# Token sums of the last group's first eight v columns added two steps later in banks of their own, gathered passes spread over four more steps, first weights loaded later

## The chip, the cores and the metric

One core of a Trainium2 chip runs the whole program. The metric is device time in microseconds (us) for one execution; the number that counts is the median of several runs. Engines are named as in the profile: PE (TensorE matmul), PEld (its weight load), DVE (VectorE), ACT (ScalarE), POOL (GpSimd), SP (SyncE, which only issues DMAs here).

## What is computed

The program is one layer of a hybrid decoder for 512 prompt tokens and 64 sample tokens, width 2048. The first half (modulation, input projection, recurrences, output projection) is not touched by the change. The second half is the expert layer: every token scores 8 heads of 128x128 product keys, takes the top 16 of 16384 experts per head, and each expert is one row of `peer_u` and one row of `peer_v`.

```python
eidx = jnp.take_along_axis(cidx, pos, axis=-1)          # 8 heads x 16 experts per token
g = jax.nn.softmax(top, axis=-1).astype(xb.dtype)
act = jax.nn.gelu(jnp.einsum('td,thkd->thk', xb, expert_u[eidx])) * g
return jnp.einsum('thk,thkd->td', act, expert_v[eidx])
...
x = x + gate2[:, None, :] * peer(h2, peer_wq, peer_sub_keys, peer_u, peer_v)
...
y_prompt = rmsnorm(xp, final_g)
```

## The kernel before: staging, queues and the order of the work

**Two ways to an expert.** The 128 blocks of 128 experts are ranked by how often the prompt uses them. The 80 most used blocks (`L = 80`) are computed densely: for every block, all 512 prompt tokens against all 128 experts, with the weight zero where a token did not choose an expert. Picks in the other blocks, and all picks of the 64 sample tokens, are *gathered*: a row of 2048 numbers per token is fetched by an indirect DMA on POOL (`take`, L1548) and DVE multiplies and adds it. The gathered picks are held as lists of columns: column j of a list holds one expert row for each of up to 128 tokens, so one *pass* is one 1 MB fetch and one DVE instruction over 128x2048 elements. There are 223 passes over `u` and 223 over `v` (lists of 64, 37, 23, 40, 33 and 26 columns, `GT`). In each `v` list DVE adds up in PSUM (`accB`, L1604), the last pass writes the finished token sums into SBUF (L1606), and an indirect DMA on POOL writes them to the DRAM tensor `accd` (L1615; the sample tokens' sums go to `accs`).

**U half.** Steps n = 0 to 159, two per dense block: PE multiplies the block's `u` weights with the tokens (24 matmuls of 512 columns a step, `u_half`, L1712). The weights come in as fp32 (`raw`, an SP DMA) and are split into a high part (`xhi`, ACT, L1202) and a low part (`xlo`, POOL, L1203); three matmuls per product follow. In the same half POOL writes the dense weights of the choice to DRAM (`gd`, L1933) and ACT writes the activations (`actd`). `E0 = 146` is the step at which the buffers of this part are handed over and the first two weight groups are read back: `load_group` (`actr`, POOL, L1654) and `load_weights` (`gsb`, POOL, L1659); DVE multiplies the two (`weigh`, L1664) and splits the product (`halve`, L1686, ACT L1682).

**V half.** The 80 dense blocks are taken in groups of 8 (nine of them) and two of 4. A step m (0 to 79) is four blocks times one quarter of the 2048 output columns, that is four columns of 128 (kq = 0 to 3), each 12 matmuls into one PSUM bank (`v_column`, L1735). There are four such banks. In a group of 8 a column needs two steps, and after the second DVE adds the bank to `acc` (`v_sum`, L1759); in the groups of 4 (steps 72 to 75 and 76 to 79) it does so after each step. Each step needs two 512 KB loads of `v` weights (SP, `raw`), two splits on ACT and POOL, and, per four blocks, one `load_weights`, `load_group`, `weigh` and `halve`. Every engine runs its queue in order, so a DVE pass that waits for its rows holds up the adds behind it, and PE then has no free bank.

**How the passes are spread.** `last` is M - VQ - ENDS = 80 - 4 - 5 = 71. The 213 `v` passes that are left after ten early ones are spread over steps 0 to 70 by a budget: every column gets room of 2.37, or 1.62 where its step ends a sum, and less in the first four steps (`room`), and `gather_to` emits as many passes as the budget has reached. Passes near a list's end count for less (down to 0.35), so they come closer together.

**The end.** At step 72 the writes to `accd` are flushed. At step 75 four rows `tok` (1 MB each) are loaded from `accd` on SP. In the last group (steps 76 to 79) each column's bank gets four more matmuls against the identity (L1739) that turn the token rows and add them, and `v_sum` then multiplies by the gate and adds (L1761), ACT squares (L1765), SP stores the column (L1766), DVE adds the square (L1771). `add_x` (L1750) adds the residual `xf` to `acc` one step ahead of that. `finish_b` (L1796 on) finishes the 64 sample tokens in pieces at the steps of `fplan`: load `tokb` and `x2b`, 16 matmuls into a PSUM tile `ph` of four banks (L1808), norm, store. After step 79 comes the final norm (`token_norm`, L1782 and L1787) and the output (L2140).

Of the kernel before, what the change touches and what calls it, by code (L numbers as in the profile page):

```python
# [81 lines left out]
def build(ctx, tc, A, O, dbg=None):  # L82
# [1640 lines left out]
    def v_column(n, gi, q, bl, first, last, kq):  # L1723
# [6 lines left out]
        for j, i in enumerate(bl):  # L1730
# [3 lines left out]
            for a, (st, mv) in enumerate(((hi, ah), (hi, al), (lo, ah))):  # L1734
                PE.matmul(pv, st, mv, start=first and j == 0 and a == 0,  # L1735
                          stop=last and not end and j == SG - 1 and a == 2)
        if end:
            for t in range(QT):
                PE.matmul(pv[:, t * 128:(t + 1) * 128], fin["tok"][t][:, k * 128:(k + 1) * 128], ident,  # L1739
                          start=False, stop=t == QT - 1)  # L1740
# [11 lines left out]
    scaled_early = (1, 4, 7, 10, 13)  # L1752

    def v_sum(gi, k, pv):
        ak = acc[:, k, :]
        if gi == 0:
            S.activation(ak, pv, AF.Copy)
        elif gi < len(GROUPS) - 1:
            V.tensor_add(ak, ak, pv)  # L1759
        else:  # L1760
            V.scalar_tensor_tensor(ak, pv, g2[:, k, 0:1], ak, op0=ALU.mult, op1=ALU.add)  # L1761
            if k == 0:
                fin["t"] = [actp.tile([128, NA], F32, name=f"sqs{i}", tag="act") for i in range(3)]
            sq = fin["t"][1]
            S.activation(sq, ak, AF.Square)  # L1765
            nc.sync.dma_start(x2d[:, k, :], ak)  # L1766
            if k == 0:
                fin["sq"] = fin["t"][0]
                V.tensor_copy(fin["sq"], sq)
            else:  # L1770
                V.tensor_add(fin["sq"], fin["sq"], sq)  # L1771
            e = k - 2 if k == KD - 1 else k - 3
            if e in scaled_early:
                S.activation(acc[:, e, :], acc[:, e, :], AF.Copy, scale=cols[:, C_FG + e:C_FG + e + 1])
# [312 lines left out]
    for m in range(M):  # L2087
# [6 lines left out]
        if m == last + 1:  # L2094
            flush(1 << 30)
        if m == last + 4:
            fin["tok"] = []
            for t in range(QT):
                r = new_row(f"tok{t}")[0]
                nc.sync.dma_start(r, accd[t * 128:(t + 1) * 128, :])  # L2100
# [177 lines left out]
```

## Time and profile before

| what | us |
|---|---|
| median of three runs | 3108.51 (3106.38 to 3116.51) |
| the profiled execution, its own time | 3115.26 |
| its span in the profile | 3113.5 |
| U half, first to last matmul of L1712 | 1141.1 to 2143.7 |
| V half, steps 0 to 71 | 2143.56 to 2974.21 |
| steps 72 to 75 | 2974.21 to 3022.42 |
| steps 76 to 79 and their token matmuls | 3022.42 to 3089.35 |
| final norm and output | 3089.35 to 3113.5 |

The profiled execution is 6.75 us above the median of the runs and inside their spread. Times in the profile count from the span's start. A step's bounds are the start of its first matmul and that of the next step's, counted off in the timeline (24 matmuls a U step, 48 a V step). Busy PE time includes the modelled ends of pipelined matmuls, so the length of a step says more than its busy share.

### The profile page before, as it was taken

The numbers are of one execution on the slowest core, as the hardware profiler recorded it, in microseconds if no ns is written. First come the engines' busy times: TensorE is split into PE (matmuls) and PEld (weight loads), VectorE is DVE, ScalarE is ACT, GpSimd is POOL, SyncE is SP. The second block draws the span as 40 slices with busy tenths as digits, with TensorE's granted clock in tenths as the row PEclk, the third lists the DMA queues.
The fourth block names the chain that finished last, engine by engine and source line by source line (L and its number), as shares of the span: only waits on it lengthen the run. The fifth ranks groups of instructions, "written<-read, shape, count | busy, mean of one in ns | idle before, by whom it ended". The sixth has DMA issues, their size and how long they took to land.

```text
span 3113.5 us, 49239 instructions
## 1 busy us (share of the span) xinstructions
PE 2996.4 (96%) x18521; PEld 2549.6 (82%) x18521; DVE 2229.6 (72%) x3414; ACT 1051.1 (34%) x1675; POOL 1764.6 (57%) x1071
## 2 busy tenths in 40 slices
PE   5899999999999999999999999989999999999997
PEld 3688888899999998877888888878887878777776
DVE  5456532144356899988899999867788898888855
ACT  3244412123243232323655655623322222122222
POOL 2133333344313336666677777768777787777842
PEclk9999999999999999999999999999999999999998
DMA  9844466644433238999879999999999997999963
GB/s 368 297 139 138 170 205 210 223 164 161 140 113 97 75 93 290 317 350 367 315 286 396 383 401 366 376 363 381 396 410 411 410 374 280 388 371 376 371 204 143
DMA packets 238900, 880.89 MB, mean 283 GB/s; under 512 B 36246, under 2 KB 37142, under 8 KB 178102
## 3 DMA queue, kind: packets, MB, share of 16 engines
q0 software_dynamic: 78096, 475.29, 38.2%
q1 hardware_dynamic: 148896, 381.17, 34.9%
q10 hardware_dynamic: 11664, 21.24, 1.8%
q8 instruction: 146, 2.39, 0.3%
q14 instruction: 98, 0.80, 0.1%
HBM read 878.84 MB, written 65.76 MB: 303 GB/s over the span
## 4 chain that ended last, share of the span: by engine, by line
PE 55%; DMA 11%; DVE 5%; issue 3%; POOL 2%; ACT 0%; SPq 0%; POOLq 0%; DVEq 0%; ACTq 0%
PE pu L1712 26%; PE pv L1735 14%; DMA raw<-vq 8%; PE pp_o L148 6%; PE qb L148 3%; PE qa L148 2%; PE gbank L1921 1%; DMA v<-v,rows 1%; DVE accB L1604 1%; POOL xlo L1203 1%; PE gx L1921 1%; DMA u<-u,rows 1%; POOL v L1548 1%; PE pv L1739 0%; DMA tok<-accd 0%
## 5 line engine op out<-in xcount | busy, mean ns | idle before, releaser
L1203 POOL TENSOR_TENSOR xlo<-raw,xhi 128x1024 fp32r<-128x1024 f32 x320 | 796.0, 2495 | 300.9 <-ACT xhi L1202 297.6
L1202 ACT ACTIVATE xhi<-raw 128x1024 fp32r<-128x1024 f32 x320 | 338.1, 1060 | 777.0 <-PE pv L1735 293.1
L1604 DVE SCALAR_TENSOR_TENSOR accB<-v,dots,accB 128x2048 f32<-128x2048 f32 x211 | 496.4, 2353 | 124.7 <-DMA v<-v,rows 122.8
L1576 DVE SCALAR_TENSOR_TENSOR u<-u,hT 128x2048 f32<-128x2048 f32 x223 | 504.1, 2283 | 103.6 <-DMA u<-u,rows 103.0
L1735 PE MATMUL pv<-ahi,xhi 128*128 128x512 f32 x1280 | 506.8, 396 | 30.1 <-DVE acc L1759 24.2
L1712 PE MATMUL pu<-hhi,xhi 128*128 128x512 f32 x1280 | 508.9, 398 | 0.7 <-ACT qt L1228 0.7
L1712 PE MATMUL pu<-hhi,xlo 128*128 128x512 f32 x1280 | 500.6, 391 | 8.8 <-POOL xlo L1203 8.8
L1735 PE MATMUL pv<-ahi,xlo 128*128 128x512 f32 x1280 | 503.2, 393 | 1.2 <-POOL xlo L1203 1.2
L1735 PE MATMUL pv<-alo,xhi 128*128 128x512 f32 x1280 | 503.5, 393 | 0.2 <-DVE alo L1686 0.2
L1712 PE MATMUL pu<-hlo,xhi 128*128 128x512 f32 x1280 | 500.9, 391 | 0.0
L1548 POOL DMA_INDIRECT u<-u,rows x223 | 226.8, 1017 | 166.3 <-DVE u L1576 120.8
L1735 PEld LDWEIGHTS pv<-ahi,xhi 128*128 128x128 f32 x1280 | 243.4, 190 | 86.8 <-issue 16.2
L1712 PEld LDWEIGHTS pu<-hhi,xlo 128*128 128x128 f32 x1280 | 241.7, 189 | 61.6 <-POOL xlo L1203 10.5
L1548 POOL DMA_INDIRECT v<-v,rows x223 | 258.1, 1158 | 59.9 <-issue 40.9
L1712 PEld LDWEIGHTS pu<-hhi,xhi 128*128 128x128 f32 x1280 | 241.5, 189 | 56.7 <-issue 1.6
L1735 PEld LDWEIGHTS pv<-ahi,xlo 128*128 128x128 f32 x1280 | 243.2, 190 | 53.5 <-POOL xlo L1203 2.0
L1735 PEld LDWEIGHTS pv<-alo,xhi 128*128 128x128 f32 x1280 | 243.6, 190 | 50.3 <-DVE alo L1686 0.6
L1712 PEld LDWEIGHTS pu<-hlo,xhi 128*128 128x128 f32 x1280 | 241.7, 189 | 47.7
L872 POOL TENSOR_TENSOR wlo_q<-raw_q,whi_q 128x1024 fp32r<-128x1024 f32 x30 | 73.3, 2443 | 174.9 <-ACT whi_q L871 161.2
L1915 ACT ACTIVATE op<-op,it 128x128 f32<-128x128 f32 x512 | 155.2, 390 | 0.0
L1715 ACT ACTIVATE act<-pu 128x512 f32<-128x512 f32 x80 | 47.9, 598 | 296.4 <-PE pu L1712 282.8
L137 POOL TENSOR_TENSOR wlo_o<-raw_o,whi_o 128x1024 fp32r<-128x1024 f32 x31 | 75.1, 2423 | 111.8 <-ACT whi_o L135 99.2
(566 smaller groups left out, 5616.9 us busy)
## 6 DMA issues: line engine op xcount, KB each, us to landing
wa<-w_ada SPq DMA_DIRECT2D x96, 1024.0 KB, 7.0
raw<-ut SPq DMA_DIRECT2D x160, 512.0 KB, 7.8
raw<-vq SPq DMA_DIRECT2D x320, 256.0 KB, 18.8
gd<-stg POOLq DMA_DIRECT2D x64, 320.0 KB, 11.7
gsb<-gd POOLq DMA_DIRECT2D x20, 1024.0 KB, 10.3
actd<-act ACTq DMA_DIRECT2D x76, 256.0 KB, 7.8
actr<-actd POOLq DMA_DIRECT2D x19, 1024.0 KB, 13.0
raw_o<-w_out SPq DMA_DIRECT2D x32, 512.0 KB, 3.6
```

Of the source, the lines that this page charges most:

```text
L137: lo_engine(share).tensor_sub(lo, raw, r32(hi))
L148: PE.matmul(o, st, mv[pick](k), start=first, stop=last)
L872: G.tensor_sub(lo, qraw.pop(j), r32(hi))
L1202: S.activation(hi, raw, AF.Copy)
L1203: G.tensor_sub(lo, raw, r32(hi))
L1548: G.indirect_dma_start(out=out, out_offset=None, in_=src, in_offset=bass.IndirectOffsetOnAxis(ap=idx, axis=0), bounds_check=NE * 128 - 1, ...
L1576: V.scalar_tensor_tensor(r, r, 1.0, st["h"], op0=ALU.mult, op1=ALU.mult, accum_out=dots[i][:, j:j + 1])
L1604: V.scalar_tensor_tensor(st["a"], r, dots[i][:, j:j + 1], st["a"], op0=ALU.mult, op1=ALU.add)
L1712: PE.matmul(pu, st[:, kk, :], movA[mv](k), start=k == 0 and a == 0, stop=k == KD - 1 and a == 2)
L1735: PE.matmul(pv, st, mv, start=first and j == 0 and a == 0, stop=last and not end and j == SG - 1 and a == 2)
L1915: S.activation(ops[:, j0 + j, :], ops[:, j0 + j, :], AF.Copy, scale=it[2][:, b * 4 + j:b * 4 + j + 1])
L1921: PE.matmul(pg[a:a + 64, j * L:(j + 1) * L], ops[:, j0 + j, a:a + 64], wr[:, j0 + j, :], start=True, stop=True)
```

## The change: what it does

- `ENDS` goes from 5 to 1, so `last` is 75: the same 213 passes are spread over steps 0 to 74.
- `LATE_K = 8`: in the last group the first eight columns (steps 76 and 77) no longer get token matmuls; their bank is multiplied by the gate and added at once. Two steps later, beside column k (8 to 15), the token rows of column k - 8 are turned into a bank of `ph` of their own, and both columns are finished one after the other (new function `finished`).
- The `tok` loads move from the start of step 75 to step 76, kq 2; the flush of the writes to `accd` from the start of step 72 to step 75, kq 2. `fplan` moves the six pieces of `finish_b` from steps 72 to 75 to steps 75 to 77.
- The columns are squared, scaled and stored in the order 8, 0, 9, 1 and so on (`order`).
- `load_weights(0)` moves from E0 + 1 to E0 + 3.

```diff
-ENDS = 5
+ENDS = 1
+LATE_K = 8
...
-                          stop=last and not end and j == SG - 1 and a == 2)
-        if end:
+                          stop=last and not (end and k >= LATE_K) and j == SG - 1 and a == 2)
+        if end and k >= LATE_K:
             for t in range(QT):
                 PE.matmul(pv[:, t * 128:(t + 1) * 128], fin["tok"][t][:, k * 128:(k + 1) * 128], ident,
                           start=False, stop=t == QT - 1)
+            e = k - LATE_K
+            for t in range(QT):
+                PE.matmul(fin["ph"][:, kq * NA + t * 128:kq * NA + (t + 1) * 128],
+                          fin["tok"][t][:, e * 128:(e + 1) * 128], ident, start=True, stop=True)
...
-    scaled_early = (1, 4, 7, 10, 13)
+    order = [e for k in range(LATE_K, KD) for e in (k, k - LATE_K)]
+    scaled_early = [order[j] for j in (1, 4, 7, 10, 13)]
...
+        elif k < LATE_K:
+            V.scalar_tensor_tensor(ak, pv, g2[:, k, 0:1], ak, op0=ALU.mult, op1=ALU.add)
         else:
...
+            finished(k, pv)
+            b = k % (KD // VQ)
+            finished(k - LATE_K, fin["ph"][:, b * NA:(b + 1) * NA])
+
+    def finished(k, src):
+        ak = acc[:, k, :]
+        V.scalar_tensor_tensor(ak, src, g2[:, k, 0:1], ak, op0=ALU.mult, op1=ALU.add)
+        j = order.index(k)
+        if j == 0:
+            fin["t"] = [actp.tile([128, NA], F32, name=f"sqs{i}", tag="act") for i in range(3)]
+        sq = fin["t"][1]
+        S.activation(sq, ak, AF.Square)
+        nc.sync.dma_start(x2d[:, k, :], ak)
+        if j == 0:
+            fin["sq"] = fin["t"][0]
+            V.tensor_copy(fin["sq"], sq)
+        else:
+            V.tensor_add(fin["sq"], fin["sq"], sq)
...
-        for sg, o in ((0, 1), (1, 7)):
+        for sg, o in ((0, 3), (1, 7)):
...
-    fplan = {(last + 1, 2), (last + 2, 3), (last + 3, 1), (last + 3, 3), (last + 4, 1), (last + 4, 3)}
+    fplan = {(last, 3), (last + 1, 0), (last + 1, 2), (last + 2, 0), (last + 2, 1), (last + 2, 3)}
...
-        if m == last + 1:
-            flush(1 << 30)
-        if m == last + 4:
-            fin["tok"] = []
-            for t in range(QT):
-                r = new_row(f"tok{t}")[0]
-                nc.sync.dma_start(r, accd[t * 128:(t + 1) * 128, :])
-                fin["tok"].append(r)
         for kq in range(KD // VQ):
+            if (m, kq) == (last, 2):
+                flush(1 << 30)
+            if (m, kq) == (last + 1, 2):
+                fin["tok"] = []
+                for t in range(QT):
+                    r = new_row(f"tok{t}")[0]
+                    nc.sync.dma_start(r, accd[t * 128:(t + 1) * 128, :])
+                    fin["tok"].append(r)
```

Where the instructions stand is set by a scheduler from the order in which the code emits them, so three places of it follow. In the changed kernel line numbers are one higher up to the change and more behind it.

**POOL, U half, around step E0.** `gd` is the last write of the dense weights, `gsb` the first read of them, `xlo` the low parts that PE waits for, `u` gathered rows. Before:

```order
L1933 DMA gd<-stg_20286 128x5x128
L1203 TENSOR_TENSOR xlo_20745<-raw_20686,xhi_20744 128x1024
L1548 DMA u_20_20748<-u,rows_9005 128x2048
L1659 DMA gsb_20780<-gd 128x2048
L1203 TENSOR_TENSOR xlo_20788<-raw_20739,xhi_20787 128x1024
L1548 DMA u_21_20791<-u,rows_9005 128x2048
L1548 DMA u_22_20796<-u,rows_9005 128x2048
L1654 DMA actr_20826<-actd 128x2048
L1203 TENSOR_TENSOR xlo_20834<-raw_20782,xhi_20833 128x1024
```

In the changed kernel, from the same low part on:

```order
L1204 TENSOR_TENSOR xlo_20745<-raw_20686,xhi_20744 128x1024
L1549 DMA u_20_20748<-u,rows_9005 128x2048
L1204 TENSOR_TENSOR xlo_20786<-raw_20739,xhi_20785 128x1024
L1549 DMA u_21_20789<-u,rows_9005 128x2048
L1549 DMA u_22_20794<-u,rows_9005 128x2048
L1655 DMA actr_20824<-actd 128x2048
L1204 TENSOR_TENSOR xlo_20832<-raw_20780,xhi_20831 128x1024
L1549 DMA u_23_20835<-u,rows_9005 128x2048
L1660 DMA gsb_20867<-gd 128x2048
L1204 TENSOR_TENSOR xlo_20875<-raw_20826,xhi_20874 128x1024
```

The read `gsb` stood two rows behind the low part `xlo_20745`, ahead of the next low part; now it stands eight rows behind it, two low parts and three more gathers later.

**DVE, the last passes.** `accB` and `v_25` are passes of the last list, `pv` with its column the banks that are added. Before, around the end of step 71 (columns 12 to 15 of group 8) and the start of step 72 (columns 0 on of group 9):

```order
L1604 SCALAR_TENSOR_TENSOR accB_27369<-v_24_28070,dots_20213,accB_27369 128x2048
L1606 SCALAR_TENSOR_TENSOR v_25_28088<-v_25_28088,dots_20213,accB_27369 128x2048
L1664 TENSOR_TENSOR actr_27905<-actr_27905,gsb_27809 128x2048
L1759 TENSOR_TENSOR acc<-acc,pv_12_28075 128x512
L1759 TENSOR_TENSOR acc<-acc,pv_13_28093 128x512
L1759 TENSOR_TENSOR acc<-acc,pv_14_28108 128x512
L1686 TENSOR_TENSOR alo_28177<-actr_27905,ahi_28176 128x2048
L1759 TENSOR_TENSOR acc<-acc,pv_15_28124 128x512
L1759 TENSOR_TENSOR acc<-acc,pv_0_28246 128x512
L1759 TENSOR_TENSOR acc<-acc,pv_1_28260 128x512
```

In the changed kernel, steps 73 to 75 of group 9 (columns 6 and 7, 8 to 11, 12):

```order
L1765 TENSOR_TENSOR acc<-acc,pv_6_28346 128x512
L1605 SCALAR_TENSOR_TENSOR accB_27651<-v_21_28230,dots_20213,accB_27651 128x2048
L1765 TENSOR_TENSOR acc<-acc,pv_7_28365 128x512
L1765 TENSOR_TENSOR acc<-acc,pv_8_28405 128x512
L1605 SCALAR_TENSOR_TENSOR accB_27651<-v_22_28263,dots_20213,accB_27651 128x2048
L1765 TENSOR_TENSOR acc<-acc,pv_9_28420 128x512
L1605 SCALAR_TENSOR_TENSOR accB_27651<-v_23_28322,dots_20213,accB_27651 128x2048
L1765 TENSOR_TENSOR acc<-acc,pv_10_28435 128x512
L1605 SCALAR_TENSOR_TENSOR accB_27651<-v_24_28341,dots_20213,accB_27651 128x2048
L1607 SCALAR_TENSOR_TENSOR v_25_28360<-v_25_28360,dots_20213,accB_27651 128x2048
L1765 TENSOR_TENSOR acc<-acc,pv_11_28453 128x512
L1765 TENSOR_TENSOR acc<-acc,pv_12_28493 128x512
```

The last pass `v_25` stood ahead of the adds of step 71; now it stands in step 74, ahead of the add of column 11. Nine passes, `v_17` to `v_25`, stand behind the first add of step 72, where there were none.

**SP, the last loads.** `raw` are `v` weights, `tok` the token rows, `tokb` and `x2b` the inputs of `finish_b`, `xf` the residual. Before, at step 75:

```order
L1191 DMA raw_28523<-vq 128x512
L2100 DMA tok_28532<-accd 128x2048
L2100 DMA tok_28534<-accd 128x2048
L2100 DMA tok_28536<-accd 128x2048
L2100 DMA tok_28538<-accd 128x2048
L1819 DMA y<-x2b 2048x1x64
L1746 DMA xf_28590<-x1d 128x4x512
```

In the changed kernel, at steps 75 and 76:

```order
L1192 DMA raw_28484<-vq 128x512
L1814 DMA tokb<-accs 128x2048
L1819 DMA x2b<-x1d 128x16x64
L1751 DMA xf_28545<-x1d 128x4x512
L1176 TENSOR_LOAD blk
L1192 ISA
L1192 DMA raw_28570<-vq 128x512
L1176 TENSOR_LOAD blk
L1192 ISA
L1192 DMA raw_28570<-vq 128x512
L2116 DMA tok_28630<-accd 128x2048
L2116 DMA tok_28632<-accd 128x2048
```

The four token rows stood behind the last weights but one; now they stand behind the last weights, and `tokb`, which had been loaded in step 72, stands ahead of those. On PE the 16 matmuls of `ph` from `tokb` stood between columns 6 and 7 in step 73; now they stand between the last column of step 75 and the first of step 76. On ACT the last high parts (`xhi`) stood between the squares of the last group; now all stand ahead of the first square.

More of the change, by code (lines that the diff above doesn't have):

```diff
@@ L1759, in v_sum @@
             V.tensor_add(ak, ak, pv)
-        else:
[L1761 to L1774, printed above, removed]
+        elif k < LATE_K:
+            V.scalar_tensor_tensor(ak, pv, g2[:, k, 0:1], ak, op0=ALU.mult, op1=ALU.add)
+        else:
+            finished(k, pv)
[15 more added lines that the diff above has]
+            V.tensor_add(fin["sq"], fin["sq"], sq)
+        e = order[j - 2 if j == KD - 1 else j - 3] if j >= 3 else None
+        if e in scaled_early:
+            S.activation(acc[:, e, :], acc[:, e, :], AF.Copy, scale=cols[:, C_FG + e:C_FG + e + 1])
     def token_norm(sq, n, nm, pool, banks):
@@ L1805, in finish_b @@
         yield
-        ph = psum["p"].tile([128, D], F32, name="ph", tag="hT", bufs=1)
+        ph = fin["ph"] = psum["p"].tile([128, D], F32, name="ph", tag="hT", bufs=1)
         for k in range(KD):
@@ L2133, in build @@
     R = drive(token_norm(fin["sq"], NA, "a", vp, banks))
-    for k in range(KD):
+    for k in order:
         ak = acc[:, k, :]
```

## The prediction

> **What bounds the kernel now.** I read the page first (the busy slices), then the windows of the V half step by step, then who waited for whom in it, then the timeline around the two stretches that the change touches beside it, and the chain at the end. From the page:
>
> ```profile
> PE   5899999999999999999999999989999999999997
> DMA  9844466644433238999879999999999997999963
> ```
>
> PE looks full nearly everywhere, and DMA is full from slice 23 to 33, which is the V half. Busy PE hides waits, so the lengths of steps decide. Windows (length, then busy time and count of PE, PEld, DVE, ACT and POOL, granted clock, DMA share, GB/s) over steps 0 to 71, steps 4 to 7, 16 to 19, 44 to 47, 64 to 67, 72 to 75 and 76 to the last matmul:
>
> ```profile
> 2143.56:2974.21 830.65, 799.18 (x3457) 654.60 (x3456) 700.63 (x385) 197.26 (x185) 640.95 (x401) 0.99 0.96 375
> 2188.46:2231.98 43.52, 43.52 (x194) 36.04 (x192) 30.43 (x13) 16.32 (x18) 36.54 (x23) 1.00 0.99 384
> 2319.00:2365.00 46.00, 43.91 (x194) 35.99 (x193) 40.35 (x21) 9.94 (x9) 36.26 (x23) 1.00 1.02 411
> 2636.26:2691.30 55.04, 46.57 (x193) 36.71 (x192) 46.64 (x27) 11.65 (x12) 41.61 (x27) 0.95 0.97 369
> 2885.33:2930.69 45.36, 44.00 (x192) 35.97 (x193) 43.17 (x26) 12.50 (x11) 37.14 (x25) 1.00 1.01 406
> 2974.21:3022.42 48.21, 48.21 (x229) 39.94 (x228) 24.22 (x32) 12.03 (x14) 21.49 (x10) 1.00 0.61 191
> 3022.42:3089.35 66.93, 61.80 (x321) 52.65 (x319) 36.18 (x44) 16.79 (x24) 15.10 (x6) 0.95 0.48 165
> ```
>
> An undisturbed step takes 43.52 / 4 = 10.88 us. Steps 0 to 71 took 830.65 where 72 x 10.88 = 783.4 would do: 47.3 us lost. Of the eighteen windows of four steps, ten are over 45 us long, spread from steps 16 to 19 to steps 64 to 67 (the first and the last are quoted, and the longest); the others are at the floor or within 1.4 us of it. Why PE stands, from the waits of PE and DVE over that stretch (us in total, times, longest), and the passes and adds themselves from the groups by line (count, busy, mean ns, idle before):
>
> ```profile
> PE pv L1735 <- DVE acc L1759: 24.2, 12, 5.1
> ```
> ```profile
> DVE accB L1604 <- DMA v<-v,rows: 116.9, 83, 5.8
> ```
> ```profile
> L1604 DVE SCALAR_TENSOR_TENSOR accB<-v,dots,accB 128x2048 f32<-128x2048 f32 x204 | 480.0, 2353 | 118.7 <-DMA v<-v,rows 116.9
> L1759 DVE TENSOR_TENSOR acc<-acc,pv 128x512 f32<-128x512 f32 x127 | 84.3, 679 | 5.9 <-PE pv L1735 5.6
> ```
>
> DVE is busy for 700.63 us and waits 116.9 us for gathered rows: together 817.5 of 830.65. PE waits for the adds, the adds stand behind passes, passes wait for rows, and rows wait for a DMA that runs at a share of 1.02. So passes per step are what this stretch is paid in. In steps 72 to 75, where no pass is left, DVE is free for 24 of 48 us and DMA at 0.61.
>
> **Part 1: nine passes leave steps 0 to 71.** The budget gives 4 x 2.37 = 9.48 to a step that ends no sum and 6.48 to one that does; over 71 steps that is 558.5, and the four new ones (71 to 74, all ending a sum) add 25.9. 213 x 25.9 / 584.4 = 9.4 passes; in the order it is nine, `v_17` to `v_25`. A pass costs DVE 2.353 us plus 116.9 / 204 = 0.57 us of waiting, 2.93 us. Were all nine on the path, 26.3 us would go. But in eight of eighteen windows PE lost little or nothing, so a pass less is worth nothing there: 26.3 x 10 / 18 = 14.6. From below: near a list's end passes come closer together, and it is these bursts that make the longest windows. By the budget the ten long windows hold 123 passes before, and 121 after, because the bursts fall on other steps: 2 x 2.93 = 6 us. I take **-15** (6 to 26): the even part of the load falls everywhere, and DVE's queue carries over from step to step. Nothing is paid for the nine at their new place: 9 x 2.353 = 21 us of passes in steps 72 to 74 meet 24 us of idle DVE, and `finish_b` and its DVE work have left as well; without that cover it would be up to the 26 again.
>
> **Part 2: the first weights.** Windows of the U steps 149, 150 and 151 (the last undisturbed, 5.44 us), then the timelines of POOL and of ACT there:
>
> ```profile
> 2070.81:2080.73 9.92, 7.37 (x26) 5.57 (x25) 6.66 (x7) 1.06 (x1) 4.12 (x3) 0.83 0.82 321
> 2080.73:2094.60 13.87, 8.06 (x26) 6.13 (x24) 6.37 (x7) 1.65 (x2) 9.78 (x8) 0.75 0.77 281
> 2094.60:2100.04 5.44, 5.44 (x26) 4.51 (x24) 3.71 (x4) 1.06 (x1) 4.95 (x4) 1.00 0.86 307
> ```
> ```profile
> 2070.63 0.91 POOL L1933 DMA_DIRECT2D gd<-stg  x1
> 2071.56 2.36 POOL L1203 TENSOR_TENSOR xlo<-raw,xhi 128x1024 fp32r<-128x1024 f32 x1
> ...
> 2084.15 0.56 POOL L1659 DMA_DIRECT2D gsb<-gd  x1 [9.04 <-DMA gd<-stg]
> 2084.73 2.36 POOL L1203 TENSOR_TENSOR xlo<-raw,xhi 128x1024 fp32r<-128x1024 f32 x1
> ```
> ```profile
> 2074.26 1.06 ACT L1202 ACTIVATE xhi<-raw 128x1024 fp32r<-128x1024 f32 x1 [5.79 <-DMA raw<-ut]
> ...
> 2082.50 1.06 ACT L1202 ACTIVATE xhi<-raw 128x1024 fp32r<-128x1024 f32 x1 [0.98 <-DMA raw<-ut]
> ```
>
> POOL stood 9.04 us at the read `gsb`, until `gd` had landed, with the next low part behind it: its high part was ready at 2075.3, it ran at 2084.73. Step 150 lost 13.87 - 5.44 = 8.4 us by that. In the new order two low parts and three gathers come first; the second of these waits for the high part of 2082.50, so POOL reaches `gsb` at about 2087, after the 2084.15 at which `gd` was there. The wait goes. What is late next is a load: the weights for step 152 are asked for when the low part of 2071.56 ends (2073.9), the ones before came in 16.5 us (asked for at 2066, there at 2082.5), so theirs are in at 2090.4, the low part 3.5 us later, where PE would be at about 2092: some 2 us. **-6.4** (-3 to -9).
>
> **Part 3: the end.** SP's timeline, the DMA issues (KB each, median us to landing), and pieces of the chain (start, us):
>
> ```profile
> 3013.12 4.04 SPq L1191 DMA_DIRECT2D raw<-vq  x4
> 3017.34 2.06 SPq L2100 DMA_DIRECT2D tok<-accd  x4
> ```
> ```profile
> xf<-x1d SPq DMA_DIRECT2D x4, 1024.0 KB, 5.2
> tok<-accd SPq DMA_DIRECT2D x4, 1024.0 KB, 10.0
> ...
> tokb<-accs SPq DMA_DIRECT2D x1, 1024.0 KB, 8.2
> ```
> ```profile
> 2993.41 3.52 PE ph L1808 x32
> ...
> 3018.71 12.87 DMA tok<-accd
> ...
> 3032.42 5.12 PE pv L1735 x12
> ...
> 3038.54 2.77 PE pv L1735 x12
> 3041.31 0.89 PE pv L1739 x8
> ...
> 3089.38 0.76 DVE acc L1761
> ```
>
> A column with its token matmuls takes 2.73 + 0.89 = 3.63 us, 16 of them 58.0; 66.93 - 58.0 = **8.9** us went on waiting for `tok` in step 76 and on the slow matmuls behind that wait (12 in 5.12 us, not 2.77). This goes: in the change the token rows are asked for some 4.5 us into step 76, need about 14 us (3017.34 to 3031.6), and PE wants them two steps after 76, one column in, over 24 us after its start. The 128 token matmuls stay 128, only placed in 78 and 79. `finish_b`'s PE work (3.52 and about 1 us) moves from steps 73 to 75 to 76 and 77: 0 in sum. New are three things. (a) `tokb` is now asked for behind the loads of step 75, 6.4 us after its start by the rows above (3017.34 against 3010.92), and PE's queue has its matmuls at 10.88. With 8.2 us to landing it is in at 14.6: **+3.7**; with the 5.2 of `xf`, 0.7; with the 10.0 of `tok`, 5.5. (b) the sample norm's square root stands behind two high parts on ACT at the start of step 77, and PE has a matmul for it one column in: 0 to 2 us, **+1**. (c) DVE's tail. One finished column now and its neighbours, from the timeline:
>
> ```profile
> 3042.24 0.75 DVE L1761 SCALAR_TENSOR_TENSOR acc<-pv,mod,acc 128x512 f32<-128x512 f32 x1 [0.79 <-PE pv L1739]
> ...
> 3043.08 0.63 ACT L1765 ACTIVATE sqs<-acc 128x512 f32<-128x512 f32 x1 [3.03 <-DVE acc L1761]
> ...
> 3043.74 0.69 DVE L1771 TENSOR_TENSOR sqs<-sqs,sqs 128x512 f32<-128x512 f32 x1 [0.76 <-ACT sqs L1765]
> 3044.35 0.75 DVE L1750 SCALAR_TENSOR_TENSOR acc<-acc,mod,xf 128x512 f32<-128x512 f32 x1
> ```
>
> A column occupies DVE from 3042.24 to 3044.35, 2.11 us. In steps 78 and 79 PE takes 2.73 + 2 x 0.89 = 4.5 us a column, DVE two finishes, 4.2, and in step 78 also an `add_x` of 0.7: DVE falls 1.6 us behind in step 78 and regains 1.2 in step 79. After PE's last matmul one finish is left as before, plus what the pair adds: the first of the two starts 0.9 us before PE ends and takes 2.1, so **+1.2** (0 to 4). Sum of part 3: -8.9 + 3.7 + 1 + 1.2 = **-3.0** (-8 to +3).
>
> Two rules of the Trainium skill bear on (a). The page TensorE: Matmul & The Clock Gate (Part 1) says that the array's clock falls to half once PE has idled for a window of about 3.4 us: the trace agrees where PE waited in U steps 149 and 150 (granted 0.83 and 0.75) and in the 5.12 us above; by it a wait of 3.7 us could cost another 5.12 - 2.77 = 2.4 us, and part 3 would be -0.6. The page DMA: Bandwidth & Descriptors (Anatomy of one DMA) gives about 2.0 us plus the bytes over 436 GB/s, an estimated 4.4 us for the 1 MB of `tokb`, and part 3 would be -6.7; the 8.2 us measured for this very transfer decides against it.
>
> **Sum.** -15 - 6.4 - 3.0 = -24.4. The profiled execution took 3115.26 us, 1.76 more than its span; 3115.26 - 24.4 = 3090.9. It is 6.75 above the median, which I take as run-to-run, so the same terms on the median: 3108.5 - 24.4 = **3084**.
>
> **Rivals.**
>
> - *The bursts decide, not the sum.* PE's 24.2 us on adds came in 12 waits, and the budget's 121 against 123 passes speak for it; the DMA share of 1.02 in the even windows (16 to 19, 64 to 67) against it. Part 1 is 0: 3108.5 - 9.4 = 3099.
> - *All nine passes count*, and `tokb` comes in time: DVE's 817.5 of 830.65 us speaks for it, the windows at the floor against it. -26.3 - 8.4 - 6.7 = -41.4: 3067.
> - *Slower: the nine passes wait at the end.* In steps 72 to 75 every step ends a sum, so PE needs all four adds within a step, and each now stands behind passes; POOL's write to `accd`, with two low parts behind it, waits for the last pass as well. If each pass waits the longest time seen, 5.8 us, 52 us of waiting meet 24 us of idle DVE: +28 us of standing PE. Rows that are so late pay nothing earlier either (part 1 is 0): 3108.5 - 9.4 + 28 = 3127. It turns slower from a mean wait of (24 + 9.4) / 9 = 3.7 us; the mean of the 83 waits is 1.4, and DMA has room there (0.61).
> - *That the change does not do what it says* is excluded by the order: passes, token matmuls and loads stand where the text puts them.
>
> **The numbers.** Forecast 0.67, bursts 0.16, all nine 0.12, slower 0.05. The range 3070 to 3102 takes in the bursts' case and leaves out the two ends. A difference under 0.3% (9.3 us, about the spread of the three runs) can't be told from none. Faster by more than that (under 3099.2): the forecast but for its upper end, all nine, and half the bursts' case: 0.81. Within it 0.14, slower 0.05.
>
> **What the profile after would show.** Right: the windows over steps 0 to 71 together some 15 us shorter, at the same 10.88 us floor; no `gsb` wait on POOL, U step 150 under 8 us; steps 72 to 75 at about 43.5 us; no wait for `tok` in the last group, a wait of PE before the `ph` matmuls of `tokb`, steps 78 and 79 at 18.1 us each. Wrong: long windows of the same total length on other steps; DVE waiting over 3 us a pass in steps 72 to 74; PE waiting for `tok` in step 78; DVE over 5 us behind PE at the end.

## The result, and the profile after

The changed kernel took 3088.05 us (median of five runs, 3086.14 to 3096.41), the kernel before beside it 3108.51 (five runs, 3103.28 to 3116.51): a ratio of 0.9935, with a 95% interval of 0.9913 to 0.9957. The forecast was 3084. The profiled execution took 3086.14 us, 1.9 below its median; its span is 3084.3 where that of before is 3113.5. Of these 29.2 us, 7.7 lie ahead of U step 146, where the change touches nothing (that step began at 2053.43 us before and at 2045.74 now; over the kernels below at 2042.03 to 2048.21). The profile of before was a late one, by about as much as the 6.75 us that it stands above its median.

The page of the changed kernel:

```profile
PE   5999999999999999999999999999999999989996
DMA  9844566654333227999879999999999998999973
```

PE is as full as before, so again the lengths of steps decide. Windows of the changed kernel (length, then busy time and count of PE, PEld, DVE, ACT and POOL, granted clock, DMA share, GB/s): U steps 149, 150 and 151; V steps 0 to 3; 4 to 71; 72 to 75 without their last 10.90 us; those 10.90; steps 76, 77 and 78; step 79 with the last token matmuls.

```profile
2062.06:2070.31 8.25, 5.74 (x26) 4.43 (x25) 5.40 (x6) 1.06 (x1) 7.50 (x5) 1.00 0.89 345
2070.31:2075.75 5.44, 5.44 (x26) 4.50 (x25) 2.30 (x2) 1.66 (x2) 0.99 (x1) 1.00 0.69 269
2075.75:2087.73 11.98, 7.27 (x25) 5.56 (x24) 9.10 (x8) 1.06 (x1) 8.98 (x8) 0.86 0.83 300
2131.25:2177.07 45.82, 44.22 (x194) 35.81 (x193) 34.19 (x17) 14.97 (x17) 36.45 (x21) 1.00 1.02 406
2177.07:2939.20 762.13, 748.16 (x3266) 617.05 (x3264) 630.69 (x359) 183.46 (x169) 595.73 (x375) 0.99 0.98 380
2939.20:2982.85 43.65, 43.65 (x193) 35.77 (x191) 40.16 (x34) 8.49 (x8) 27.16 (x15) 1.00 0.67 223
2982.85:2993.75 10.90, 7.08 (x34) 6.85 (x33) 2.51 (x2) 1.06 (x1) 5.01 (x2) 0.62 1.05 346
2993.75:3005.99 12.24, 12.24 (x53) 9.80 (x52) 9.71 (x11) 2.40 (x3) 0.50 (x1) 0.92 0.91 367
3005.99:3021.53 15.54, 13.29 (x52) 10.47 (x51) 10.07 (x15) 3.56 (x5) 4.86 (x3) 0.89 0.00 0
3021.53:3039.51 17.98, 17.98 (x113) 16.07 (x112) 12.19 (x18) 5.47 (x8) 5.08 (x2) 1.00 0.56 176
3039.51:3058.00 18.49, 18.43 (x115) 16.29 (x113) 12.43 (x19) 6.89 (x11) 0.00 (x0) 1.00 0.31 114
```

The same stretches of the kernel before: from U step 146 to the V half, V steps 0 to 3, steps 4 to 71.

```profile
2053.43:2143.56 90.13, 81.32 (x338) 65.61 (x336) 64.98 (x46) 20.76 (x23) 64.81 (x43) 0.94 0.90 348
2143.56:2188.46 44.90, 44.13 (x194) 35.88 (x192) 30.49 (x15) 14.75 (x17) 34.93 (x22) 1.00 1.01 397
2188.46:2974.21 785.75, 755.05 (x3265) 618.71 (x3264) 670.15 (x371) 182.51 (x168) 606.02 (x379) 0.98 0.95 373
```

**Steps 4 to 71** went from 785.75 to 762.13 us, 23.6 less; their floor is 68 x 10.88 = 739.8. What PE waits for in steps 0 to 71 of the changed kernel (us in total, times, longest), and what DVE waits for there:

```profile
PE pv L1736 <- ACT xhi L1203: 11.4, 3, 7.3
PE pv L1736 <- DVE acc L1765: 2.6, 2, 2.4
```
```profile
DVE accB L1605 <- DMA v<-v,rows: 103.2, 68, 4.0
DVE acc L1765 <- PE pv L1736: 33.9, 24, 2.0
```

Before, PE waited 24.2 us for DVE's adds. Now it waits 2.6, and it is DVE that waits 33.9 us for PE.

**The hand-over from U to V.** POOL's timeline in the changed kernel:

```profile
2070.52 0.99 POOL L1549 DMA_INDIRECT u<-u,rows  x1 [0.60 <-DVE u L1577]
2078.08 0.56 POOL L1655 DMA_DIRECT2D actr<-actd  x1 [6.57 <-DMA gd<-stg]
2078.66 2.36 POOL L1204 TENSOR_TENSOR xlo<-raw,xhi 128x1024 fp32r<-128x1024 f32 x1
```

The wait at `gsb` is gone, and the read that now comes first, `actr`, stands in its place: 6.57 us, with a low part behind it. By the profile it stood for the same last `gd` write, which had been issued at 2061.84 and took 15.9 us to land; why a read of `actd` should wait for it the profile does not say. So step 150 is undisturbed (5.44) and step 151 takes 11.98.

**The end.** PE's timeline at step 76 and in step 77, then POOL's and DVE's in step 77 and at the end, and the waits from step 72 on:

```profile
2986.93 7.06 PE L1823 MATMUL ph<-both,tokb 128*128 128x64 f32 x32 [3.82 <-DMA tokb<-accs]
2993.75 0.77 PE L1736 MATMUL pv<-ahi,xhi 128*128 128x512 f32 x1
...
3011.27 0.43 PE L1802 MATMUL ph<-ident,rcfb 64*128 64x64 f32 x2 [2.25 <-DVE rcfb L159]
...
3012.96 0.63 PE L1736 MATMUL pv<-ahi,xlo 128*128 128x512 f32 x1
```
```profile
3005.49 5.16 POOL L1204 TENSOR_TENSOR xlo<-raw,xhi 128x1024 fp32r<-128x1024 f32 x2 [17.63 <-ACT xhi L1203]
...
3006.56 1.89 DVE L1755 SCALAR_TENSOR_TENSOR acc<-acc,mod,xf 128x512 f32<-128x512 f32 x1
...
3008.97 1.70 DVE L156 TENSOR_TENSOR rcfb<-rcfb 64x1 f32<-64x1 f32 x1
3010.70 0.15 DVE L157 TENSOR_TENSOR rcfb<-rcfb 64x1 f32<-64x1 f32 x1
...
3061.10 0.69 DVE L1786 TENSOR_TENSOR sqs<-sqs,sqs 128x512 f32<-128x512 f32 x1 [0.76 <-ACT sqs L1780]
```
```profile
DVE sqs L1786 <- ACT sqs L1780: 11.4, 15, 0.8
...
PE ph L1823 <- DMA tokb<-accs: 3.8, 1, 3.8
```

No matmul waits for `tok` any more, and from step 72 on DVE's waits name no gathered row. But PE waits 3.82 us for `tokb`, runs the `ph` matmuls at half the clock (7.06 us, not 3.52; granted 0.62 over these 10.90 us), waits 2.25 us in step 77 for the sample norm (`rcfb`), and DVE ends 3.8 us behind PE's last matmul (3061.79 against 3057.94). That norm was late on DVE: the `add_x` ahead of it took 1.89 us and one of its small operations 1.70, both while POOL split the last two low parts; with POOL idle they took 0.74 (at 3004.33) and 0.15 (in e3). Without these 2.7 us more, an estimate from the rows, PE would not have waited there. From step 72 to the end of the span it is 145.1 us now and 139.3 before.

### The profile page after: what moved, and what is told of

It reads as the page before. It is cut to its first block, busy times and chain, and to the rows that moved or that the text cites. A ratio compares the mean times of both kernels' runs of the same rounds, so it can differ in the third digit from the quotient of the medians.

```text
span 3084.3 us, 49250 instructions
## 1 busy us (share of the span) xinstructions
PE 2985.5 (97%) x18521; PEld 2546.3 (83%) x18521; DVE 2217.9 (72%) x3422; ACT 1052.3 (34%) x1675; POOL 1760.1 (57%) x1071
## 4 chain that ended last, share of the span: by engine, by line
PE 62%; DVE 5%; DMA 5%; issue 3%; POOL 2%; ACT 1%; SPq 0%; POOLq 0%; DVEq 0%; ACTq 0%
PE pu L1713 24%; PE pv L1736 23%; PE pp_o L149 6%; PE qb L149 3%; PE qa L149 2%; DMA u<-u,rows 2%; DMA v<-v,rows 2%; PE gbank L1936 1%; PE gx L1936 1%; POOL xlo L1204 1%; DMA raw<-vq 1%; DVE accB L1605 1%; POOL u L1549 1%; PE qab L149 0%; PE sc L1026 0%
## 5 line engine op out<-in xcount | busy, mean ns | idle before, releaser
L1736 PE MATMUL pv<-ahi,xhi 128*128 128x512 f32 x1280 | 503.9, 394 | 14.0 <-ACT xhi L1203 11.4
L1736 PEld LDWEIGHTS pv<-ahi,xhi 128*128 128x128 f32 x1280 | 242.8, 190 | 67.5 <-ACT xhi L1203 15.9
## 6 DMA issues: line engine op xcount, KB each, us to landing
gsb<-gd POOLq DMA_DIRECT2D x20, 1024.0 KB, 11.4
```

Of the source, the lines that this page charges most:

```text
L1736: PE.matmul(pv, st, mv, start=first and j == 0 and a == 0, stop=last and not (end and k >= LATE_K) and j == SG - 1 and a == 2)
```

## The experiments

The theory after the two traces: (1) a pass that leaves steps 4 to 71 is worth its whole price there, wherever the stalls show; (2) the first weights' later load moves the wait from one read to the next; (3) the end got longer, since `tokb` is late and what follows hangs on it. The rivals: the 23.6 us are the bursts or run-to-run; the U half's gain is real; the end is bound by DVE's 16 finished columns.

A step's place is read as in the table of before. The stretches in each kernel's profile, in us (the last is reckoned with the span rounded to 0.1):

| kernel | 146 to V half | V steps 0 to 3 | V steps 4 to 71 | 72 to the end | median | the kernel before beside it | ratio, 95% interval |
|---|---|---|---|---|---|---|---|
| before | 90.1 | 44.9 | 785.8 | 139.3 | | | |
| the changed kernel | 85.5 | 45.8 | 762.1 | 145.1 | 3088.05 | 3108.51 | 0.9935 (0.9913 to 0.9957) |
| e1, part 2 alone | 85.0 | 48.9 | 786.0 | 137.6 | 3106.70 | 3109.52 | 0.9990 (0.9981 to 0.9999) |
| e2, part 1 undone | 84.2 | 52.6 | 785.7 | 144.0 | 3110.24 | 3109.52 | 1.0001 (0.9991 to 1.0011) |
| e3, ph later | 83.9 | 45.7 | 763.4 | 141.8 | 3081.85 | 3109.52 | 0.9912 (0.9899 to 0.9926) |
| e4, reads later | 79.2 | 53.0 | 761.7 | 144.0 | 3086.66 | 3109.52 | 0.9927 (0.9913 to 0.9940) |
| e5, pieces apart | 85.9 | 51.5 | 761.4 | 137.4 | 3082.32 | 3109.59 | 0.9908 (0.9892 to 0.9924) |
| e6, half of part 1 | 85.0 | 46.2 | 775.6 | 145.3 | 3101.75 | 3109.59 | 0.9976 (0.9965 to 0.9987) |
| e7, weigh earlier | 85.8 | 47.8 | 761.7 | 143.5 | 3084.38 | 3109.59 | 0.9918 (0.9905 to 0.9932) |
| e8, squares apart | 85.4 | 52.0 | 763.0 | 143.3 | 3085.55 | 3109.59 | 0.9924 (0.9910 to 0.9937) |
| e9b, tokb early | 84.5 | 52.5 | 760.9 | 131.0 | 3077.37 | 3107.36 | 0.9905 (0.9887 to 0.9922) |
| e9, tokb and xf early | 84.6 | 51.8 | 761.8 | 132.5 | 3076.96 | 3107.36 | 0.9898 (0.9880 to 0.9916) |
| e10, one step more | 85.7 | 52.0 | 759.8 | 136.8 | 3076.86 | 3107.36 | 0.9900 (0.9882 to 0.9917) |
| e11, part 2 undone | 89.5 | 44.8 | 762.4 | 145.4 | 3090.03 | 3110.12 | 0.9934 (0.9922 to 0.9946) |

**Part 1 undone (e2), and half of it (e6).**

```diff
-ENDS = 1
+ENDS = 5
...
-    last = M - VQ - ENDS
+    last, end_m = M - VQ - ENDS, M - VQ - 1
```

The budget ends at step 70 again (in e6, `ENDS = 3`, at step 72); the flush, `tok` and `fplan` count from `end_m` and stay where the change has them.

> The changed kernel with part 1 alone undone: the passes are spread over steps 0 to 70 again, all else stays where the change has it. By the prediction (9 passes x 2.93 us x 10/18 of the windows) it is 15 us above the changed kernel, 3103. If all nine passes count and more of the stall goes with them, as the windows of the changed kernel show (807.95 us for 830.65), 23 us above, 3111. By the rival that only the bursts decide, and that the 22.7 us were run-to-run, no difference from the changed kernel. In steps 72 to 75 there is no pass again; apart from the wait for tokb and the matmuls behind it they take 43.5 us as in the changed kernel (43.7), if the passes cost nothing there.

> The changed kernel with half of part 1: the passes spread over steps 0 to 72 (ENDS 3 for the budget alone, all else where the change has it). e2 (steps 0 to 70) and the changed kernel (steps 0 to 74) differ by 22 us. If a pass costs the same wherever the load stands (2.5 us each), it lies halfway, 3099. If DVE's queue is what binds steps 0 to 71 until its load falls under that of PE, and the changed kernel is already past that point (PE's waits for the adds fell from 24.2 to 2.6 us), the first half brings more than the second: 3093 to 3096. If only the bursts near a list's end count, that fall on other steps in each of them, no order is to be expected: anything from 3088 to 3112.

The windows of steps 4 to 71, of e2 and of e6, and e2's waits of PE in steps 0 to 71:

```profile
2180.99:2966.69 785.70, 753.33 (x3265) 618.79 (x3264) 664.83 (x369) 181.33 (x168) 606.86 (x379) 0.98 0.95 371
```
```profile
2175.93:2951.49 775.56, 752.89 (x3266) 616.48 (x3265) 646.16 (x365) 183.81 (x169) 592.08 (x378) 0.99 0.96 376
```
```profile
PE pv L1736 <- DVE acc L1765: 27.1, 9, 7.1
```

With the passes back, e2 is the kernel before again in this stretch: 785.7 us, and 27.1 us of PE's waits for the adds. It took 3110.24 us, 22 above the changed kernel by the medians (20.5 by the two ratios): the spreading is the whole of what the change gained, and not run-to-run. Over all kernels the stretch takes 785.7 to 786.0 us with the passes in it and 760.9 to 763.4 without (e10, one step further, aside). e6 lies 10.1 us below e2 and 13.4 above the changed kernel. By the starts of the passes in DVE's timeline, steps 4 to 71 hold 204 of them before, 203 in e2, 199 in e6 and 194 in the changed kernel: 2.5 us a pass from e2 to e6, 2.7 from there to the changed kernel. So neither "the first half brings more" nor "only the bursts" holds; the price runs about straight.

**The multiply earlier (e7).** In all groups from the third on:

```diff
-        jobs.setdefault(h_ - 2, []).append(lambda sg=sg: weigh(sg))
+        jobs.setdefault(h_ - 4, []).append(lambda sg=sg: weigh(sg))
```

> The changed kernel with the multiply weigh two columns (5.4 us) earlier before its split, in all groups from the third on. What is left of waiting in steps 0 to 71 of the changed kernel is 11.4 us for high parts, 7.35 of them in one place, step 55, where ACT stands 11.3 us at the split's first half until DVE has done the multiply behind a list's end; steps 52 to 55 lost 7.6 us in the kernel before as well. If that is so, step 55 goes to under 13 us and 5 to 9 us are gained: 3079 to 3083. If DVE then stands at the multiply for the loads (11 to 12 us to landing, 13.6 us before it at the least), with the adds behind it, it loses up to 10 us: 3098. If the last loss is the bursts themselves, no difference.

The waits of PE in steps 0 to 71 of e7, and its window of steps 4 to 71:

```profile
PE pv L1736 <- DVE acc L1765: 13.5, 6, 3.8
...
PE pv L1736 <- ACT xhi L1203: 1.0, 1, 1.0
```
```profile
2180.70:2942.41 761.71, 747.05 (x3266) 615.09 (x3264) 638.11 (x361) 183.82 (x169) 598.10 (x375) 0.99 0.97 380
```

The expected stall went: the wait for high parts fell from 11.4 to 1.0 us, and steps 52 to 55 lost 1.4 us, not 7.6. And it brought nothing: the waits for adds rose from 2.6 to 13.5, and the stretch took 761.7 us for 762.1. The median is 3.7 us lower than the changed kernel's, which the intervals of the two ratios do not hold apart. A stall taken away at one place came back at others.

**Part 2 alone (e1), undone (e11), and two steps further (e4).** e1 is the kernel before, e11 the changed kernel:

```diff
-        for sg, o in ((0, 1), (1, 7)):
+        for sg, o in ((0, 3), (1, 7)):
```

(e11 turned round). In e4:

```diff
-        if n - E0 == 2:
+        if n - E0 == 4:
             load_group(0)
-        for sg, o in ((0, 3), (1, 7)):
+        for sg, o in ((0, 5), (1, 9)):
...
-        if n - E0 == 6:
+        if n - E0 == 8:
             weigh(0)
```

> The kernel before with one edit of the change alone: load_weights(0) at E0 + 3. By the prediction's part 2 the POOL wait of 9.04 us at gsb goes and step 150 (13.87 us before) is undisturbed: 6.4 us less than before, 3102, with 3 to 9 us of room. By what the profile of the changed kernel shows, the wait only moves, from gsb to the read actr that now comes first on POOL (6.57 us there): steps 146 to 159 take 85.5 us, not 90.1, some 4.6 us less, 3104, and one U step near 12 us stays. If the change of 4.6 us was run-to-run, there is no difference. Steps 0 to 71, which this kernel shares with the kernel before, give a second reading of their 830.65 us: if the 22.7 us by which the changed kernel was shorter there is the spreading, it is within 3 us of 830; if it is run-to-run, it is nearer 815.

> The changed kernel with part 2 alone undone: load_weights(0) at E0 + 1 again. By the prediction's price of part 2 it is 6.4 us slower than the changed kernel: 3094.5; by the 4.6 us between the two profiles from step 146 to the V half, 3092.7; by e1, whose median was 2.8 us under the kernel before, 3091. If what the U half no longer loses is lost in V steps 0 to 3 (which took 44.9 to 53.0 us over the kernels so far), there is no difference, 3088, and from step 146 to V step 3 it takes 130 to 137 us like the others, however step 150 comes out.

> The changed kernel, with the first reads back of activations and dense weights two steps later still (load_group(0) at E0 + 4, load_weights(0) at E0 + 5, the multiply and the split two steps later with them, load_weights(1) at E0 + 9). If POOL's wait for the last gd write (6.57 us at actr) is what made step 151 11.99 us long, POOL reaches actr some 11 us later, after that write has landed, and 6.5 us go: 3081.5, steps 149 to 152 without a stall but for about 2.8 us in step 149. If the raw weight loads are late by themselves (the prediction's 2 us), 4 us. If the wait is passed on to a later reader (DVE's multiply, the next weights), no gain or a loss of up to 5 us in steps 155 to 159.

From U step 146 to the V half and V steps 0 to 3, in e1, e11 and e4:

```profile
2042.55:2127.51 84.96, 78.34 (x338) 64.08 (x337) 59.80 (x45) 20.89 (x23) 64.72 (x43) 0.98 0.93 361
2127.51:2176.45 48.94, 45.72 (x193) 37.09 (x192) 38.41 (x17) 14.85 (x17) 35.76 (x21) 0.97 1.02 396
```
```profile
2045.92:2135.41 89.49, 79.62 (x337) 64.96 (x336) 64.24 (x46) 20.77 (x23) 64.58 (x42) 0.94 0.88 344
2135.41:2180.19 44.78, 44.17 (x193) 35.88 (x192) 29.21 (x15) 14.63 (x17) 34.79 (x21) 1.00 1.01 397
```
```profile
2043.35:2122.55 79.20, 76.74 (x337) 62.91 (x336) 56.24 (x42) 20.52 (x23) 63.44 (x42) 1.00 0.93 370
2122.55:2175.57 53.02, 47.46 (x194) 37.84 (x193) 39.01 (x19) 15.21 (x18) 37.04 (x22) 0.94 1.01 393
```

In the U half the gain is there every time: 90.1 and 89.5 us with the old place, 83.9 to 85.9 with the new one, 79.2 in e4, where POOL reaches `actr` late enough and no step is long but 149 (7.55) and 153 (6.38). In V steps 0 to 3 some or all of it is given back: 44.9 and 44.8 with the old place, 45.7 to 52.6 with the new, 53.0 in e4. Both together take 135.0 and 134.3 with the old place, 129.6 to 137.6 with the new (mean of eleven kernels 134.8), and 132.2 in e4. By the medians part 2 is worth 2.8 us in e1 (0.3 to 5.9 by its interval, so just more than nothing) and 2 in e11, where the two ratios differ by 0.3 us and their intervals overlap. That a wait moved to `actr` is shown by the rows above; why steps 0 to 3 give the time back is only argued: DMA runs at a share of 1.01 or 1.02 in them in every kernel quoted, so that what V needs there would not come earlier just because PE starts earlier.

**The end: ph later (e3), the pieces apart (e5).** On the changed kernel:

```diff
-    fplan = {(last, 3), (last + 1, 0), (last + 1, 2), (last + 2, 0), (last + 2, 1), (last + 2, 3)}
+    fplan = {(last, 3), (last + 1, 2), (last + 1, 3), (last + 2, 0), (last + 2, 1), (last + 2, 3)}
```

and in e5 `{(last, 3), (last + 1, 2), (last + 2, 0), (last + 2, 2), (last + 2, 3), (last + 3, 0)}`.

> The changed kernel, with the 32 ph matmuls two columns (5.4 us) later, at step 76, kq 2, and the piece behind them one column later; the load of tokb stays. The wait of 3.82 us at tokb should go. By the prediction's price of (a) the gain is that wait, 3.7 us: 3084. If the halved clock behind the wait counts as well (ph matmuls 7.06 us, not 3.52, and the next few V matmuls slow), it is 3.8 + 3.5 + 0.7 = 8 us: 3080. If the end is bound elsewhere (DVE's chain of 16 columns from 3025 us on, the load of the last xf), little is gained: within 2 us of the changed kernel.

> The changed kernel with the pieces of finish_b further apart: the ph matmuls at step 76, kq 2 as in e3, the sum of squares at 77, kq 0, its matmul at 77, kq 2, the norm's matmul at 77, kq 3, the last multiply and the store at 78, kq 0. In e3 the wait moved to the matmul on sqb (6.18 us, and 12 matmuls at 0.43 us, not 0.227, behind it). If that is all that e3 left, 6.2 + 2.4 = 8.6 us go from e3's 3081.9: 3073. If DVE, which stood 5.73 us for the last but two xf load, is what binds steps 76 and 77, half of it comes back at the norm's matmul: 3077.5. If DVE's chain of 16 finished columns binds the end (it gets 1.2 us more work in step 78), nothing is gained over e3: 3082.

PE's waits from step 72 on in e3, then the windows of steps 72 to 75, 76, 77 and 78 of e5:

```profile
PE ph L1797 <- DVE sqb L1830: 6.2, 1, 6.2
```
```profile
2945.38:2988.90 43.52, 43.52 (x193) 36.04 (x192) 37.32 (x32) 8.50 (x8) 25.71 (x15) 1.00 0.65 225
2988.90:3003.40 14.50, 14.50 (x81) 12.58 (x80) 8.39 (x9) 2.82 (x3) 5.01 (x2) 1.00 1.07 381
3003.40:3018.69 15.29, 12.05 (x53) 9.34 (x52) 12.82 (x18) 3.98 (x6) 5.52 (x3) 1.00 0.66 251
3018.69:3037.91 19.22, 18.85 (x113) 16.29 (x112) 14.53 (x17) 5.47 (x8) 4.95 (x2) 1.00 0.33 98
```

In e3 the wait for `tokb` was gone, and 6.18 us stood at the matmul on `sqb` instead: DVE had waited 5.73 us for an `xf` load that SP asks for right behind `tokb`, with its four operations on `x2b` behind that. e3 still gained 6.2 us in the median, 3.3 of them at the end by its profile. In e5 the end takes 137.4 us, 7.7 less than in the changed kernel: step 76 is clean, step 77 keeps 4.4 us (2.41 of them at `sqb`), and step 78, with the multiply on `x2b` in it, is 1.2 longer. Its median shows none of that over e3; its V steps 0 to 3 took 51.5 us, not 45.7, in the profile.

**The squares apart (e8), the loads early (e9b, e9), one step more (e10).** In e8 a column's square is added only after the next column's multiply, with two tiles in turn:

```diff
-        sq = fin["t"][1]
+        if j >= 2:
+            V.tensor_add(fin["sq"], fin["sq"], fin["t"][1 + (j - 1) % 2])
+        sq = fin["t"][1 + j % 2] if j else fin["t"][0]
...
```

e9b has that, and the six pieces at

```diff
-    fplan = {(last, 3), (last + 1, 0), (last + 1, 2), (last + 2, 0), (last + 2, 1), (last + 2, 3)}
+    fplan = {(last - 1, 3), (last + 1, 0), (last + 1, 2), (last + 2, 0), (last + 2, 2), (last + 2, 3)}
```

e9 also calls `load_x(1)` at step 74, kq 3. e10 has `ENDS = 0`, `tok` at step 77, kq 0, and the pieces at steps 75 to 78.

> The changed kernel with two tiles for the squares in turn, and each square added to the sum after the next column's multiply, so that DVE no longer stands 0.76 us for ACT in each of 16 finished columns (2.11 us each from 3029 to 3062 us). If DVE's chain sets the end, DVE then follows PE (4.5 us a pair against 1.4 x 2 + 0.7), and its end comes from 3.8 us behind PE's last matmul to about 2: 1.6 us less, 3086.4. If PE sets it and the tail is fixed, no difference. Either is under what the runs' medians can tell; the trace has to show it.

> The changed kernel with the loads of finish_b (tokb, x2b) one step earlier on SP, ahead of the loads for step 75, its ph matmuls at step 76, kq 0 as the change has them, the pieces behind them at 76 kq 2, 77 kq 0, 77 kq 2 and 77 kq 3, and the squares apart as in e8. From the start of step 72 to the end of the span the changed kernel and those with the same end took 143.5 to 145.3 us, e5 137.4. If the wait for tokb (3.8), the half clock behind it (3.5 + 0.7) and the stall of step 77 (4.4) were all due to tokb's late arrival, and the squares give 1.1, about 13 us go: some 131, 3075. If the xf load, asked for at the same time, still holds DVE up (4.6 us in e5), the wait turns up at sqb: 136, 3080. If row slots for tokb are not free that early, SP stands there with the loads of step 75 behind it: slower than the changed kernel.

> As e9b, with the second xf load one step earlier too, so that tokb, x2b and two xf loads are asked for before the loads of step 75. If DVE's wait for that xf load (5.73 us in e3, 4.58 in e5) is what makes sqb late, it is 0 to 5 us faster than e9b: 129 to 131 us from step 72 to the end, 3073 to 3075. If the 3.5 MB ahead of the loads of step 75 make those late instead (at 400 GB/s they take 8.8 us), step 75 or 76 stands for up to 5 us, and it is slower than e9b.

> The changed kernel with the passes spread over one step more still (steps 0 to 75), the tok loads at step 77, kq 0, the pieces of finish_b a step later (loads at 75 kq 3, ph at 76 kq 2, then 77 kq 0, 77 kq 2, 77 kq 3, 78 kq 0) and the squares apart. If a pass that leaves steps 4 to 71 is worth 2.4 us wherever the load stands (785.8 us with 0 moved, 775.6 with 5, 762.2 with 10), the two or three that leave now bring 5 to 7: 755 to 757 us for steps 4 to 71. If the changed kernel has reached a floor of another kind there (PE's waits for adds are 2.6 us, 11.4 are for high parts behind the split on ACT), 762 again. The end goes as in e5, 137 us; if tok, asked for 13.6 us before PE wants it, is late, step 78 stands 1 to 5 us more. Altogether 3074 to 3078, or 3081 if the passes bring nothing.

DVE's end in e8; the windows of steps 72 to 75, 76 with `ph`, 77 and 78 of e9b; steps 4 to 71 of e10:

```profile
3065.50 0.75 DVE L1775 SCALAR_TENSOR_TENSOR acc<-ph,mod,acc 128x512 f32<-128x512 f32 x1
3066.16 0.68 DVE L1780 TENSOR_TENSOR sqs<-sqs,sqs 128x512 f32<-128x512 f32 x1
3067.00 0.69 DVE L1786 TENSOR_TENSOR sqs<-sqs,sqs 128x512 f32<-128x512 f32 x1 [0.16 <-ACT sqs L1783]
```
```profile
2939.93:2983.45 43.52, 43.52 (x193) 36.05 (x192) 38.43 (x32) 8.50 (x8) 25.73 (x16) 1.00 0.74 242
2983.45:2998.25 14.80, 14.80 (x84) 12.59 (x82) 13.09 (x14) 3.46 (x4) 5.91 (x3) 1.00 0.95 359
2998.25:3009.90 11.65, 11.65 (x52) 9.33 (x51) 10.36 (x15) 3.56 (x5) 5.16 (x3) 1.00 0.47 188
3009.90:3027.89 17.99, 17.99 (x114) 16.08 (x112) 12.00 (x17) 5.47 (x8) 5.08 (x2) 1.00 0.54 176
```
```profile
2180.17:2939.93 759.76, 746.09 (x3265) 613.95 (x3264) 629.88 (x359) 183.71 (x169) 600.50 (x373) 1.00 0.97 379
```

e8 ends 2.6 us behind PE, not 3.8; its end of 143.3 us is 1.1 under the mean of the five kernels with the old squares (the changed one, e2, e4, e6 and e7: 144.4). In e9b PE stands nowhere between step 72 and the final norm, every step is at its floor, and the end takes 131.0 us as expected, 14.1 less than in the changed kernel: theory (3) holds, and with the squares apart DVE's finished columns held PE up nowhere. e9's second early load adds nothing (3076.96 against 3077.37). e10 has one pass fewer in steps 4 to 71 than the changed kernel (193) and is 2.4 us shorter there, less than the 5 to 7 expected, since two or three were to leave; at its end PE waited 2.0 us at `ph`, in 136.8 us. All three are some 11 us under the changed kernel in the median, and some 30 under the kernel before; that the 14 us of e9b are not all in its median fits with V steps 0 to 3, 52.5 us in its profile and 45.8 in the changed kernel's.

## Why the prediction was right, and where its steps were not

The forecast was 24.4 us less; by the medians it was 20.5. The direction and the cause were right. Two terms were off by 9 us each, on opposite sides, so that the sum came closer than its parts, by luck.

- **Part 1: -15 forecast, -23.6 measured** (steps 4 to 71; e2: 22 us by the medians). The mechanism was right: passes are what this stretch is paid in, and PE's waits for the adds went with them. The step that failed is the weighting by 10 of 18 windows, on the ground that "a pass less is worth nothing there". e6 and e7 show that the passes set the length of the whole stretch, and not of single windows: a pass is worth 2.4 to 2.7 us wherever the stalls show, nearer to the 2.93 that the same text had worked out than to the 1.7 that the weighting left of it. The rival "all nine passes count" had the better price.
- **Nothing paid at the new place:** right. Steps 72 to 75 took 43.65 us without `tokb`'s wait, and no wait for a row stands among DVE's there. The slower rival's wait of 3.7 us a pass did not come.
- **Part 2: -6.4 forecast, about 0 to -3 by the medians.** `gsb`'s wait went, and step 150 was undisturbed. What was late next was not the raw load that the text named but `actr`, now the first on POOL to wait for the last `gd` write, 6.57 us. Of the 4.6 us gained in the U half V steps 0 to 3 gave back 0.9 in this profile and about all in the mean of eleven kernels; the text said nothing of these steps.
- **Part 3: -3.0 forecast, +5.8 measured.** The wait for `tok` went with its slow matmuls, 8.9 us, as forecast. (a) was put at 3.7, and the wait was 3.82; but the wait's price was 8.4: 3.82, plus 7.06 - 3.52 = 3.5 at half the clock, plus 1.1 in step 76 (12.24 - 10.88, less 0.3 for two small matmuls that are in it). The row that should have carried this stood in the text: 12 matmuls in 5.12 us behind the wait for `tok`. By the rule of the Trainium skill named there (TensorE: Matmul & The Clock Gate, Part 1) part 3 would have been -0.6: the trace agrees that the clock fell behind this wait (0.62), and the price was some 2 us higher still. `tokb` took 8.7 us to land, where (a) reckoned with 8.2. (b) was put at 1 and cost 4.3 (15.54 - 10.88, less 0.4 for the matmuls themselves): 2.25 of waiting and for the most part slow matmuls behind it. Its mechanism was wrong as well: the square root on ACT held DVE up for 0.27 us, and what came late was DVE, slowed beside POOL's low parts. (c) was put at 1.2; from PE's last matmul to the end of the span it is 26.4 us, not 24.2. Together -8.9 + 8.4 + 4.3 + 2.2 = 6.0, for the 5.8 of the two spans.
- **What was to be seen:** steps 78 and 79 at 18.1 us (17.98 and 18.49), no wait for `tok`, a wait before `ph`: right. DVE more than 5 us behind PE at the end: no, 3.8.

What stays open: whether a pass is paid as DVE's time (2.35 us) or as its fetch's time on DMA (1 MB at the 380 GB/s of this stretch is an estimated 2.8 us), since both leave with it in every run; what holds the last 22 us over the floor in steps 4 to 71 of the changed kernel, where DVE waits 33.9 us for PE and yet a removed stall brings nothing; and what sets how much of the U half's gain V steps 0 to 3 keep (45.7 to 52.6 us with the same code there).

## What to carry to other kernels

In a stretch where one engine's work and its feed fill the time, price an operation at its whole cost over the stretch, not by the share of windows in which stalls can be seen; taking a stall away at one place only moves it. Cost a wait of PE with what follows it, the slow matmuls at the lower clock as well, and look for a row in the profile that shows how many there are. Where a wait is removed by reordering, name the next instruction in that queue that can wait for the same write.

## What the runs showed of the hardware

- The clock fell after shorter waits than the 3.82 us above too, and not always. In the changed kernel PE waited 2.25 us in step 77, and from 1.7 us after it had started again its matmuls came every 0.43 us for 3.1 us; in e5 a wait of 2.41 us left the step's clock at 1.00. In the kernel before, PE waited 1.95 us until 2411.59, and from 2413.01 to 2416.42 the granted clock was 0.50; behind a wait of 2.76 us until 2885.33 it was 1.00. Of the waits of the kernel before in which the prediction found its rule to agree, that of 5.8 us in U step 150 was long enough for it, but that in step 149 was 2.6 us and the longest in step 76 was 2.8. The Trainium skill (TensorE: Matmul & The Clock Gate, Part 1) gives a free-running window of some 3.4 us of idling; the 1.95 and 2.25 us are shorter than that, so here the measurement decides: a shorter wait can be followed by it, and where the wait falls seems to matter, which no run tested.
- A small DVE operation with two inputs in SBUF, `rcfb` at 64x1, took 1.70 us in the changed kernel while POOL split a low part (3005.49 to 3010.65 us), and its neighbours of the same size 0.15; in e3, with POOL idle, the same operation took 0.15. The Trainium skill (SBUF — State Buffer, Who interferes with whom) says that such an instruction and one of GpSimd shut each other out for a whole instruction; the row agrees.
- On SP an issue took time by itself: the `xf` load behind four `raw` loads, `tokb` and `x2b` held SP for 7.20 us (2979.29 to 2986.49) in the changed kernel, the others 0.38 to 1.24. The weight loads behind it in the queue were issued only at 2987.07.
